# A hybrid attention step on one Trainium2 core: group A's decode is given fewer projection steps, group A's attention more; the token sums start two steps later and their tiles lie in another order

## The chip, the core and the metric

The kernel runs on one core of one Trainium2 chip. The core has five engines that work side by side, each through its own list of instructions in order: TensorE (PE; its weight loads are listed apart as PEld), VectorE (DVE), ScalarE (ACT), GpSimd (POOL) and SyncE (SP), which here issues the DMA transfers. They wait for each other by semaphores. The metric is the time of one execution on the device in microseconds (us), lower is better. Before the change it is 1755.42 us, the median of three runs (1755.3 to 1756.09).

## What is computed

One layer of a streaming encoder, on 1024 prompt tokens and on 8 requests of 16 new tokens each, which bring 1024 past tokens of cache. Everything is float32.

```python
qkv = rmsnorm(x) @ w_in                       # columns: q, k, v of group A, then of group B
# group A, 8 heads x 64: stick-breaking attention over the whole past
log_keep = where(causal, log_sigmoid(-z), 0)  # z = q k / 8
w = exp(log_sigmoid(z) + cumsum_from_the_right(log_keep) - log_keep)
# group B, 8 heads x 64: softmax over the own chunk and 8 chunks before, with a bias by distance
x = x + concat(rmsnorm(a), rmsnorm(b)) @ w_out
x = x + (silu(h @ w_gate) * (h @ w_up)) @ w_down
x = x + sigmoid(rmsnorm(x) @ w_ple_gate) * (p @ w_ple_proj)
```

Outputs are the two results and the new keys and values of both groups.

## The kernel before

Products of float32 are made from two parts: a number is split into a rounded high part (a cast on ACT) and the rest (a subtraction on DVE or POOL), and each product is three matmuls: high x high, high x low, low x high. The 1152 tokens are nine tiles of 128: eight of the prompt, one of all new tokens.

The program begins with the projection (`qkv`, line 265), a Python generator that yields after each small piece of work. Some weight chunks of 256 columns are done by a seven-product scheme (`seven`, line 420), which needs four sums of token blocks, T1 to T4, made by `sum_forms` (line 360) in steps on DVE; `beside` (line 492) takes three such steps after each step of the projection that runs meanwhile. When the scheme is done, its tiles are given back (`close_wide`, line 956), and what is left are 50 steps: 12 value steps of group A (`others`, line 308: one tile of tokens times 256 columns, 24 matmuls of 256 columns, a copy to a staging tile `st`, then a cast on ACT and a subtraction on POOL into `sv` and a store), 18 value steps of group B, and 20 steps of group B's queries (`queries`, line 282). The weights pass through one raw buffer, so a chunk's splitting (ACT and POOL) precedes the loading of the next.

Beside these 50 steps run two other generators.

- Group A's decode (`decode`, line 524): for each request four pieces of 256 cached keys and four of cached values, 512 KB each, 64 in all, through seven buffers `draw`. In each step one piece of keys is turned (L597) and scored (L619) and, six steps later, one piece of values is weighted (L606 turns the weights, L660 accumulates). 38 steps.
- The attention of the prompt (`attention`, line 707): 128 units, one per head and query tile; the first 64 are group A's. In a unit PE makes scores (L771, L772), ACT two sigmoids (`w` and `keep`, L774 and L775), DVE two running products over `keep` (L111 on the diagonal block, L114 on the rest), POOL the product of `w` and `keep` (L784); five units later PE turns the weights (L802), ACT and DVE split them, and PE multiplies with the values (L825, L826).

How they are interleaved is set by `advance(main, side, ratio, steps)` (line 924): after each step of `main`, `side` is advanced by `ratio` steps on average. In the decode stage PE's instructions stay in the order of the calls (a manual schedule); all other engines, and PE in the attention stage, are put in order by a scheduler that estimates times. Memory is given by stacks of pools: the decode's tiles lie where T1 to T4 and the scheme's other tiles were, and a tile's first write waits for the last reader of what lay there before. Attention's tiles follow where decode's were.

The calls that set the stages are these (lines 1014 to 1026):

```python
    with tc.manual_schedule(engines={mybir.EngineType.PE}):
        advance(project, dec, 1.5, 24 - 1)
        for _ in dec:
            pass
    ...
    att = run(range(8))
    advance(project, att, 2.25)
```

Of the kernel before, what the change touches and what calls it, by code (L numbers as in the profile page):

```python
# [14 lines left out]
F32R = mybir.dt.float32r  # L15
# [7 lines left out]
P = 128  # L23
D = 1024
KT = 8
# [14 lines left out]
def tile_hymba_step(  # L40
# [58 lines left out]
    def mm3(out, ah, al, bh, bl, start, stop):  # L99
        T.matmul(out, lhsT=ah, rhs=bh, start=start, stop=False)  # L100
        T.matmul(out, lhsT=ah, rhs=bl, start=False, stop=False)  # L101
        T.matmul(out, lhsT=al, rhs=bh, start=False, stop=stop)  # L102

    def sub(eng, out, a, hi):
        return eng.tensor_tensor(out, a, hi.bitcast(F32), op=ALU.subtract)  # L105
# [60 lines left out]
    def cols(w, c, n=256):  # L166
        return w[:, c * n : (c + 1) * n].rearrange("(k p) c -> p k c", p=P)
# [97 lines left out]
    def qkv(ch, hT, stg, first, second, wide):  # L265
# [35 lines left out]
        def rows_of(grp, c, st, t0, n):  # L301
            for pr in range(2):
                pt = ps["t"].tile([P, 384], F32, name="pt", tag="T")[:, : n * P]
                for o in range(n):
                    T_.transpose(pt[:, o * P : (o + 1) * P], st[:, o, pr * P : (pr + 1) * P], ident)
                transposed_out(grp, 1, c * 2 + pr, t0 * P, n * P, parts(n * P, pt))

        def others(grp, w, c, wts, gs):

            wh, wl = wts  # L310
            for g in gs:
                st = stg[0].tile([P, 3, 256], F32, name="st", tag="st", bufs=2)
                for o in range(3):
                    ps_ = ps["o"].tile([P, 256], F32, name="ps", tag="O")
                    for k in range(KT):
                        mm3(ps_, *hT.tok(g * 3 + o, k), wh[:, k], wl[:, k], k == 0, k == KT - 1)
                    (V.tensor_copy if o % 2 else A.copy)(st[:, o], ps_)  # L317
                    yield
                if w == 1:
                    rows_of(grp, c, st, g * 3, 3)  # L320
                else:
                    for o in range(3):
                        sv = stg[0].tile([P, 2, stg[1]], F32R, name="sv", tag="sq").rearrange("p a b -> p (a b)")[:, :512]
                        sv = sv.rearrange("p (h x d) -> p h x d", h=4, x=2)
                        flat = st[:, o].rearrange("p (h d) -> p h d", d=HD)
                        A.copy(sv[:, :, 0, :], flat)  # L326
                        sub(G, sv[:, :, 1, :], flat, sv[:, :, 0, :])
                        tok = slice((g * 3 + o) * P, (g * 3 + o + 1) * P)
                        nc.sync.dma_start(vhl[grp][c, tok, :], sv.bitcast(F32).rearrange("p h x d -> p (h x d)"))
                first = 4 if grp else 0  # L330
                ts_ = [t for t in range(g * 3, g * 3 + 3) if first <= t < NP]
                if ts_:
                    lo, hi = ts_[0], ts_[-1] + 1
                    nc.sync.dma_start(
                        kv_prompt[grp, w][0, 0, (lo - first) * P : (hi - first) * P, c * 4 : c * 4 + 4, :]
                        .rearrange("(t p) h d -> p t (h d)", p=P),
                        st[:, lo - g * 3 : hi - g * 3],
                    )
                if g == 2:
                    nc.sync.dma_start(  # L340
                        kv_sample[grp, w][0, :, :, c * 4 : c * 4 + 4, :].rearrange("b i h d -> (b i) (h d)"),
                        st[:, 2],
                    )

        ready, sums_of = {}, {}
# [6 lines left out]
        def load(grp, w, c, summed=False):  # L352
            if (grp, w, c) not in raws:
                fetch(grp, w, c)
            v = raws.pop((grp, w, c))
            ready[grp, w, c] = ch.parts(v, KT, 256, 4 if summed else 2)
            if summed:
                sums_of[grp, w, c] = weight_sums(wide["pool"], v)
# [130 lines left out]
        sums_ = sum_forms()  # L489
        load(0, 0, 0)  # L490

        def beside(main):
            for _ in main:
                for _ in range(3):
                    next(sums_, None)
                yield

        yield from beside(others(0, 1, 1, ready[0, 1, 1], range(3)))
        load(0, 0, 1, True)
        yield from beside(queries(0, 0, ready[0, 0, 0]))  # L500
        for _ in sums_:
            pass
# [409 lines left out]
    def pool(stack, name, side, bufs=1):  # L912
        return stack.enter_context(tc.tile_pool(name=name, bufs=bufs, side=side, reuse_waits="tile"))
# [10 lines left out]
    def advance(main, side, ratio, steps=None):  # L924

        due, n = 0.0, 0
        while steps is None or n < steps:
            if next(main, "end") == "end":
                break
            n += 1  # L930
            due += ratio
            while due >= 1.0:
                due -= 1.0
                next(side, None)
        return n
# [12 lines left out]
    wide, wstack = {}, ExitStack()  # L948

    def open_wide():  # L950
        fp = pool(wstack, "qforms", "left")
        wide["forms"] = {n: [fp.tile([P, KT // 2, 512], F32R, name=n + x) for x in "hl"] for n in ("T1", "T2", "T4", "T3")}
        wide["pool"] = pool(wstack, "qsums", "left")
        wide["banks"] = wstack.enter_context(tc.tile_pool(name="ps_w", bufs=3, space=PSUM, side="right", reuse_waits="tile"))

# [8 lines left out]
    with tc.tile_pool(name="x1", bufs=2, side="right") as xp, tc.manual_schedule(engines=all_engines):  # L964
# [28 lines left out]
        project = qkv(ch, hT, stg, w_first, ch.raw(cols(w_in[0], 3), KT, 256), wide)  # L993
# [18 lines left out]
    dp = pool(first, "dA", "left")  # L1012
    dec = decode(0, Chunks(dp, "d", 1024, RAWS, 2), dp)
    with tc.manual_schedule(engines={mybir.EngineType.PE}):
        advance(project, dec, 1.5, 24 - 1)
        for _ in dec:
            pass
    first.close()
# [4 lines left out]
    at = pool(left, "at", "left")  # L1023
    run, pairs, done = attention(at, ps, LAG)
    att = run(range(8))
    advance(project, att, 2.25)
    right.close()


# [2 lines left out]
    dec = decode(1, Chunks(dp, "d", 1024, RAWS - 1, 2), dp)  # L1032
    pp = ps["early"] = pool(dstack, "pp", "right", 2)

    def embed():

        with tc.issue_after(kept[-1].ins):
            wj = ch.load(w_ple_proj[0].rearrange("(k p) c -> p k c", p=P), 2, D)
        def turned(t):
            pn = pp.tile([P, 256], F32, name="pn", tag="pn")  # L1040
            nc.sync.dma_start(pn, p_tok[t])
            pt = ps["t"].tile([P, 512], F32, name="pt", tag="T")
            for j in range(2):
                T.transpose(pt[:, j * P : (j + 1) * P], pn[:, j * P : (j + 1) * P], ident)
            pT = [pp.tile([P, 2, P], F32R, name=f"pT{n}", tag=f"pT{n}", bufs=PT) for n in "hl"]
            pv = pt[:, :256].rearrange("p (k n) -> p k n", k=2)
            A.copy(pT[0], pv)
            sub(V, pT[1], pv, pT[0])
            return pT

        nxt = turned(0)
        yield
        for t in range(NT):
            pT = nxt
            for c in range(2):
                cs = slice(c * 512, c * 512 + 512)
                ps_ = ps["s"].tile([P, 512], F32, name="pj", tag="S")
                for k in range(2):
                    mm3(ps_, pT[0][:, k], pT[1][:, k], wj[0][:, k, cs], wj[1][:, k, cs], k == 0, k == 1)
                o = pp.tile([P, 512], F32, name="pjo", tag="pjo", bufs=2)  # L1060
                A.copy(o, ps_)
                nc.sync.dma_start(proj[t * P : (t + 1) * P, cs], o)
                if c == 0 and t + 1 < NT:
                    nxt = turned(t + 1)
                yield
# [5 lines left out]
    def along(a, b, ratio, due):  # L1071

        for _ in a:
            yield
            due += ratio
            while due >= 1.0:
                due -= 1.0
                if next(b, "end") != "end":
                    yield
        yield from b  # L1080
# [3 lines left out]
    beside = along(dec, embed(), 1.2, -3.0)  # L1084
# [84 lines left out]
    fp = pool(fstack, "forms", "left")  # L1169
# [10 lines left out]
    def form(name):  # L1180
        return [fp.tile([P, KT // 2, 512], F32R, name=name + n) for n in "hl"]
# [3 lines left out]
    T4, B22, B11, B21, T2, T3, T1 = [form(n) for n in ("T4", "B22", "B11", "B21", "T2", "T3", "T1")]  # L1185
# [300 lines left out]
    def act_place(n=D):  # L1486
        return [sA.tile([P, NT * P], F32R, name="act" + x, tag="act" + x, bufs=4)[:, :n] for x in "hl"]
# [104 lines left out]
    for d in range(nd):  # L1592
# [24 lines left out]
        S2, T2, S1, T1 = got  # L1617
# [21 lines left out]
        S3, T3, A4, T4 = got  # L1639
# [5 lines left out]
        else:  # L1645
            w_d = ch.parts(w_last, 2, D, 2, V)
            act = []
            for f in range(2):
                hl = act_place(NT * P)
# [281 lines left out]
```

## Time and profile before

| what | value |
|---|---|
| median of three runs | 1755.42 us |
| profiled execution | 1754.85 us |
| its span, first to last instruction | 1753.1 us |
| mean granted clock of TensorE | 0.98 |
| PE / PEld busy | 95% / 80% |
| DVE / ACT / POOL busy | 65% / 47% / 48% |
| first and last matmul that turns group A's cached keys (L597) | 220.6 and 353.4 us |
| last matmul on group A's cached values (L660) | 371.8 us |
| first scores of attention (L771) | 384.5 us |

The profile is one execution. Times within it count from its first instruction; the part of an execution outside the span is the difference of the second and third rows. A group of instructions is named by line, engine, operation and tiles (written <- read). An idle time is put down to what ended it. A busy share is an average over stages, so the stages are read one by one: from 220 to 376 us the decode of group A with projection steps between, from 391 to 495 us attention with the rest of the projection, from 495 to 600 us attention with little beside it, and from about 580 us on decode of group B.

### The profile page before, as it was taken

The page shows a single profiled execution, that of the slowest core. Times are in us where ns is not written, and L with a number is a line of the kernel's source. Part 1 is how long each engine was busy: PE and PEld are TensorE (multiplying, and loading weights), DVE is VectorE, ACT ScalarE, POOL GpSimd, SP SyncE. Part 2 cuts the span into 40 slices and gives each one's busy share as a digit, 9 for nine tenths or more (in the row PEclk, how much of TensorE's full clock was granted, in tenths as well). Part 3 has the DMA queues.
Part 4 walks back from the last instruction along what each step waited for, and adds up shares of the span by engine and source line. Part 5 has one row for each costly group of instructions (what it writes and reads, how often), then busy time and mean ns, then how long its engine had stood idle before and what let it go on. Part 6 is the DMA issues. An engine that isn't in the chain of part 4 may idle for free.

```text
span 1753.1 us, 27540 instructions
## 1 busy us (share of the span) xinstructions
PE 1668.3 (95%) x10064; PEld 1406.2 (80%) x10064; DVE 1144.3 (65%) x1810; ACT 831.5 (47%) x1763; POOL 849.9 (48%) x693
## 2 busy tenths in 40 slices
PE   8899899998977899889999999999999999999998
PEld 7888778887866678778778888888888878788887
DVE  6954134427889866765477666666666597798875
ACT  5433245526677767753474333333333244433663
POOL 2434222223566622312367555555555278967763
PEclk9999999999998899999999999999999999999999
DMA  5444779974583797675532222222222597722322
GB/s 188 152 143 163 255 252 326 307 202 144 139 233 100 222 278 230 176 215 173 168 133 72 94 93 93 93 94 93 94 94 93 190 385 260 269 81 77 128 96 97
DMA packets 176137, 293.48 MB, mean 167 GB/s; under 512 B 16897, under 2 KB 95489, under 8 KB 173698
## 3 DMA queue, kind: packets, MB, share of 16 engines
q1 hardware_dynamic: 176002, 291.72, 51.0%
q8 instruction: 80, 1.31, 0.3%
q14 instruction: 55, 0.45, 0.1%
HBM read 204.77 MB, written 86.90 MB: 166 GB/s over the span
## 4 chain that ended last, share of the span: by engine, by line
PE 72%; DMA 7%; DVE 5%; ACT 3%; POOL 3%; issue 2%; SPq 1%; POOLq 0%; ACTq 0%; DVEq 0%
PE ps L216 27%; PE ps L100 4%; PE ps L101 4%; PE ps L102 4%; PE pt L1536 4%; PE pt L216 3%; PE ps L1536 3%; PE pt L802 2%; DMA v<-sv 2%; PE pt L597 2%; DVE keep L114 1%; PE po L826 1%; PE po L825 1%; PE acc L660 1%; PE S L771 1%
## 5 line engine op out<-in xcount | busy, mean ns | idle before, releaser
L105 POOL TENSOR_TENSOR wlo<-wraw,whi 128x512 fp32r<-128x512 f32 (+1 forms) x127 | 219.0, 1747 | 106.3 <-ACT whi L159 103.2
L100 PE MATMUL ps<-whi,hTh 128*128 128x256 f32 x448 | 133.8, 299 | 8.1 <-ACT st L317 8.0
L102 PE MATMUL ps<-whi,hTl 128*128 128x256 f32 x448 | 130.2, 291 | 4.5 <-DVE hTl L105 4.5
L101 PE MATMUL ps<-wlo,hTh 128*128 128x256 f32 x448 | 129.8, 290 | 0.0
L159 ACT CAST whi<-wraw 128x512 fp32r<-128x512 f32 (+1 forms) x124 | 87.1, 718 | 74.7 <-PE ps L216 30.8
L784 POOL TENSOR_TENSOR w<-w,keep 128x127 f32<-128x127 f32 (+4 forms) x64 | 78.2, 1224 | 76.7 <-DVE keep L114 51.1
L802 PE MATMUL pt<-ident,w 128*128 128x128 f32 x528 | 91.3, 293 | 20.5 <-POOL w L784 8.5
L105 DVE TENSOR_TENSOR wtl<-pt,wth 128x512 fp32r<-128x512 f32 (+1 forms) x192 | 94.3, 512 | 17.9 <-ACT wth L806 17.7
L806 ACT CAST wth<-pt 128x512 fp32r<-128x512 f32 (+1 forms) x192 | 84.3, 465 | 35.8 <-PE pt L802 34.9
L100 PEld LDWEIGHTS ps<-whi,hTh 128*128 128x128 f32 x448 | 88.9, 199 | 14.8 <-ACT st L317 8.6
L114 DVE TENSOR_TENSOR_SCAN keep<-keep,zero 128x128 f32<-128x128 f32 (+7 forms) x64 | 97.9, 1531 | 1.3
L802 PEld LDWEIGHTS pt<-ident,w 128*128 128x128 f32 x528 | 65.8, 148 | 35.7 <-POOL w L784 11.4
L102 PEld LDWEIGHTS ps<-whi,hTl 128*128 128x128 f32 x448 | 88.8, 198 | 5.1 <-DVE hTl L105 5.0
L771 PE MATMUL S<-qk 128*128 128x384 f32 (+2 forms) x192 | 76.3, 400 | 14.6 <-ACT keep L775 11.5
L101 PEld LDWEIGHTS ps<-wlo,hTh 128*128 128x128 f32 x448 | 89.0, 199 | 0.4 <-issue 0.2
L825 PE MATMUL po<-wth,vk 128*128 128x256 f32 (+1 forms) x304 | 79.3, 292 | 0.4 <-DVE wtl L105 0.2
L105 POOL TENSOR_TENSOR actl<-actr,acth 128x1024 fp32r<-128x1024 f32 (+1 forms) x22 | 61.4, 2792 | 32.2 <-DMA sr<-acts 20.7
L826 PE MATMUL po<-wtl,vk 128*128 128x256 f32 (+1 forms) x304 | 74.2, 288 | 0.0
L598 DVE COPY kT<-pt 128x512 f32<-128x512 f32 x48 | 33.0, 687 | 59.7 <-PE pt L597 54.9
L105 POOL TENSOR_TENSOR S3l<-s,S3h 128x512 fp32r<-128x512 f32 x24 | 32.4, 1350 | 76.0 <-ACT S3h L236 67.9
L105 POOL TENSOR_TENSOR S2l<-s,S2h 128x512 fp32r<-128x512 f32 x24 | 35.3, 1469 | 64.8 <-PE ps L216 35.4
L105 POOL TENSOR_TENSOR sv<-st,sv 128x256 fp32r<-128x256 f32 x36 | 26.3, 734 | 79.3 <-ACT sv L326 69.5
(500 smaller groups left out, 5617.0 us busy)
## 6 DMA issues: line engine op xcount, KB each, us to landing
draw<-in_cache_sb_k SPq DMA_DIRECT2D x32, 512.0 KB, 6.7
draw<-in_cache_sb_v SPq DMA_DIRECT2D x32, 512.0 KB, 5.4
act<-sg SPq DMA_DIRECT2D x11, 1152.0 KB
actr<-act SPq DMA_DIRECT2D x22, 576.0 KB, 5.8
wraw<-in_w_in SPq DMA_DIRECT2D x11, 1024.0 KB
wraw<-in_w_gate SPq DMA_DIRECT2D x11, 1024.0 KB, 5.5
wraw<-in_w_up SPq DMA_DIRECT2D x11, 1024.0 KB
v<-sv SPq DMA_DIRECT2D x36, 256.0 KB, 5.3
```

Of the source, the lines that this page charges most:

```text
L100: T.matmul(out, lhsT=ah, rhs=bh, start=start, stop=False)
L101: T.matmul(out, lhsT=ah, rhs=bl, start=False, stop=False)
L102: T.matmul(out, lhsT=al, rhs=bh, start=False, stop=stop)
L105: return eng.tensor_tensor(out, a, hi.bitcast(F32), op=ALU.subtract)
L114: V.tensor_tensor_scan(rev, rev, zero[:, 0:1].to_broadcast([P, n - d]), keep[:, n - d : n - d + 1], op0=ALU.mult, op1=ALU.max)
L159: A.copy(h[:, o], v[:, o])
L216: T.matmul(out, lhsT=a[x][:, k], rhs=b[y][:, k], start=(not more and k == 0 and n == 0), stop=(k == 3 and n == 2), skip_group_check=more)
L771: T.matmul(sc, lhsT=hd["qq"][:, qs], rhs=hd["kkh"][:, kc], start=True, stop=False)
L802: T.transpose(pt[:, (c - c0) * P : (c - c0 + 1) * P], w[:, c * P : (c + 1) * P], ident)
L825: T.matmul(dst, lhsT=vs, rhs=wth[:, kb - base, c0:c1], start=(i == 0), stop=False)
L826: T.matmul(dst, lhsT=vs, rhs=wtl[:, kb - base, c0:c1], start=False, stop=(i == nkb - 1))
L1536: T.matmul(out, lhsT=a[i][:, x, m * P : (m + 1) * P], rhs=b[j][:, x], start=(not more and x == 0 and n == 0), stop=(x == 1 and n == 2), sk ...
```

## The change

Four edits. The first call of `beside` leaves out the token sums after its first two steps. The tiles of T1 to T4 are allocated in the order T2, T3, T1, T4, the order in which the scheme reads them. The decode of group A runs beside 11 projection steps in place of 23, at 3.2 decode steps to each in place of 1.5. The attention runs beside what is then left, 38 steps in place of 26, at 1.54 units to each in place of 2.25. No computation is added or left out.

```diff
-        def beside(main):
-            for _ in main:
-                for _ in range(3):
+        def beside(main, idle=0):
+            for n, _ in enumerate(main):
+                for _ in range(3 if n >= idle else 0):
                     next(sums_, None)
                 yield
 
-        yield from beside(others(0, 1, 1, ready[0, 1, 1], range(3)))
+        yield from beside(others(0, 1, 1, ready[0, 1, 1], range(3)), 2)
...
-        wide["forms"] = {n: [fp.tile([P, KT // 2, 512], F32R, name=n + x) for x in "hl"] for n in ("T1", "T2", "T4", "T3")}
+        wide["forms"] = {n: [fp.tile([P, KT // 2, 512], F32R, name=n + x) for x in "hl"] for n in ("T2", "T3", "T1", "T4")}
...
-        advance(project, dec, 1.5, 24 - 1)
+        advance(project, dec, 3.2, 12 - 1)
...
-    advance(project, att, 2.25)
+    advance(project, att, 1.54)
```

In the lists of instructions, everything up to the start of the decode stands as before on all engines. From there they differ. First ACT's list at the start of the decode, before and then changed (`st` is the staging of a projection step, `sv` its split values, `kT` turned keys of the cache, `qbd` the decode's queries, `wdec` its scores):

```order
L326 CAST sv_2006<-st_1919 128x4x64
L317 COPY st_2012<-ps_2065 128x256
L326 CAST sv_2091<-st_2012 128x4x64
L588 COPY qbd0_2208<-sq0_2181 64x4x16 x2
L588 COPY qbd1_2209<-sq0_2181 64x4x16 x2
L326 CAST sv_2095<-st_2012 128x4x64
L326 CAST sv_2099<-st_2012 128x4x64
L317 COPY st_2112<-ps_2113 128x256
```

```order
L317 COPY st_2012<-ps_2065 128x256
L326 CAST sv_2091<-st_2012 128x4x64
L598 COPY kT_2216<-pt_2217 128x4x128
L588 COPY qbd0_2208<-sq0_2181 64x4x16 x2
L588 COPY qbd1_2209<-sq0_2181 64x4x16 x2
L598 COPY kT_2231<-pt_2232 128x4x128
L621 ACT_TABLE_LOAD
L621 ACTIVATE wdec_2214<-sdec_2244 128x256
```

The first turned keys and scores of the decode now stand ahead of the last value casts and of the next projection step's copy, which came first before.

Next SP's list in the middle of the decode, before and then changed (`draw` is a piece of cache, `v0` the store of a value step, `mixs0` the decode's output, `out_3` the new values):

```order
L329 DMA v0_78<-sv_3084 128x512
L141 DMA draw_2931<-in_cache_sb_v 128x2x512
L141 DMA draw_2966<-in_cache_sb_k 128x2x512
L329 DMA v0_78<-sv_3088 128x512
L141 DMA draw_2968<-in_cache_sb_v 128x2x512
L141 DMA draw_3041<-in_cache_sb_k 128x2x512
L141 DMA draw_3043<-in_cache_sb_v 128x2x512
L678 DMA mixs0_111<-ow_3006 8x16x64
L334 DMA out_3<-st_2828 128x3x256
```

```order
L329 DMA v0_78<-sv_3394 128x512
L141 DMA draw_2990<-in_cache_sb_v 128x2x512
L141 DMA draw_3025<-in_cache_sb_k 128x2x512
L141 DMA draw_3027<-in_cache_sb_v 128x2x512
L141 DMA draw_3100<-in_cache_sb_k 128x2x512
L141 DMA draw_3102<-in_cache_sb_v 128x2x512
L678 DMA mixs0_111<-ow_3065 8x16x64
L141 DMA draw_3143<-in_cache_sb_k 128x2x512
L329 DMA v0_78<-sv_3398 128x512
```

Between two stores of values there are now six pieces of cache, before two to four.

Last DVE's list where the projection ends, before and then changed (L275 splits the queries' last sums, L111 opens a unit of attention, `wtl` is the low part of turned weights):

```order
L275 SCALAR_TENSOR_TENSOR sq_6641<-ps_6534,sq_6641 128x256
L841 TENSOR_REDUCE osb_5616<-pt_5624 128x4x64
L111 SCALAR_TENSOR_TENSOR keep_5541<-keep_5541,ident_60 128x128
L275 SCALAR_TENSOR_TENSOR sq_6646<-ps_6534,sq_6646 128x256
L114 SCALAR_TENSOR_TENSOR keep_5541<-keep_5541,zero_68 128x768
```

```order
L275 SCALAR_TENSOR_TENSOR sq_6641<-ps_6573,sq_6641 128x256
L105 TENSOR_TENSOR wtl_6323<-pt_6331,wth_6322 128x128
L111 SCALAR_TENSOR_TENSOR keep_6258<-keep_6258,ident_60 128x128
L105 TENSOR_TENSOR wtl_6323<-pt_6383,wth_6322 128x4x128
L105 TENSOR_TENSOR wtl_6323<-pt_6390,wth_6322 128x2x128
L111 SCALAR_TENSOR_TENSOR keep_6373<-keep_6373,ident_60 128x128
L275 SCALAR_TENSOR_TENSOR sq_6646<-ps_6573,sq_6646 128x256
```

The L111 ahead of the last L275 is the 31st of group A's 64 in the list before, and the 50th in the changed one.

## The prediction

> **What bounds the kernel now.** I read the page first (TensorE, PE, is busy 95% of the span), then cut the stretch in which the change acts into stages and asked for each engine's busy time in each. Columns: stretch, its length, busy time of each engine with its instructions, granted TensorE clock, share of the DMA engines, GB/s.
>
> ```profile
> span 1753.1 us, 27540 instructions
> PE 1668.3 (95%) x10064; PEld 1406.2 (80%) x10064; DVE 1144.3 (65%) x1810; ACT 831.5 (47%) x1763; POOL 849.9 (48%) x693
> ...
> 210.00:225.00 15.00, 8.25 (x54) 7.43 (x55) 1.81 (x3) 5.64 (x14) 6.50 (x8) 0.77 0.72 233
> 225.00:255.00 30.00, 27.23 (x263) 22.61 (x262) 9.98 (x15) 15.97 (x42) 8.70 (x8) 0.94 0.72 231
> 255.00:360.00 105.00, 104.25 (x1267) 90.71 (x1270) 49.40 (x79) 53.58 (x152) 26.85 (x37) 1.00 0.94 319
> 360.00:376.00 16.00, 16.00 (x204) 14.41 (x203) 3.26 (x10) 4.92 (x16) 4.23 (x7) 1.00 0.21 70
> 376.00:391.00 15.00, 15.00 (x95) 13.57 (x94) 1.98 (x4) 4.55 (x10) 7.48 (x8) 1.00 0.99 232
> 391.00:495.00 104.00, 97.67 (x619) 85.36 (x617) 81.46 (x125) 67.64 (x170) 45.34 (x67) 0.97 0.53 149
> 495.00:600.00 105.00, 81.72 (x515) 67.94 (x516) 97.11 (x144) 78.59 (x192) 68.12 (x86) 0.85 0.64 176
> ```
>
> From 255 to 360 us, group A's decode with projection steps between, PE is busy 104.25 of 105 us and the DMA engines run at 0.94: PE sets the pace, and the DMA queue is close behind. From 391 to 495, attention with the rest of the projection between, PE is again the fullest (97.67 of 104) with VectorE (DVE) at 81.46. From 495 to 600 the projection is used up: DVE is busy 97.11 of 105, PE 81.72 at a granted clock of 0.85. So time that PE lacks in the first two stages lies unused in the third, 105 - 81.72 = 23.3 us, and the 6.3 us of the second. Moving PE work from decode into attention is worth something only as far as it lands in that idle time.
>
> **The change part by part.** *One projection step.* In the decode stage the pieces are these (start and duration of PE instructions):
>
> ```profile
> 266.55 0.39 PE L100 MATMUL ps<-whi,hTh 128*128 128x256 f32 x1
> ...
> 269.41 0.28 PE L102 MATMUL ps<-whi,hTl 128*128 128x256 f32 x1
> 269.53 1.04 PE L597 MATMUL pt<-ident,draw 128*128 128x128 f32 x8
> 270.40 0.38 PE L606 MATMUL pt<-ident,wdec 128*128 128x128 f32 x2
> 270.72 0.67 PE L619 MATMUL sdec<-kT,qbd 128*32 128x272 f32 x8
> 271.20 0.62 PE L660 MATMUL acc<-draw,wt 128*32 128x128 f32 x16
> 271.75 0.38 PE L100 MATMUL ps<-whi,hTh 128*128 128x256 f32 x1
> ```
>
> A projection step of 24 matmuls takes 269.53 - 266.55 = 2.98 us, a decode step 271.75 - 269.53 = 2.22 us. The old ratio, 1.5 decode steps to a projection step, puts 23 projection steps beside the decode; the new, 3.2, puts 11. Twelve steps leave: 12 x 2.98 = 35.8 us of a stage that PE fills. First term: **-35.8 us**.
>
> *The DMA queue in that stage.* With fewer projection steps the cache is asked for faster. What each step moves:
>
> ```profile
> draw<-in_cache_sb_k SPq DMA_DIRECT2D x32, 512.0 KB, 6.7
> draw<-in_cache_sb_v SPq DMA_DIRECT2D x32, 512.0 KB, 5.4
> ...
> v<-sv SPq DMA_DIRECT2D x36, 256.0 KB, 5.3
> out<-st SPq DMA_DIRECT2D x8, 384.0 KB, 4.4
> ...
> L100 PE MATMUL ps<-whi,hTh 128*128 128x256 f32 x133 | 39.3, 295 | 0.0
> L619 PE MATMUL sdec<-kT,qbd 128*32 128x256 f32 (+1 forms) x192 | 15.5, 394 | 0.1
> ```
>
> The last two rows are for 255 to 360 us: 133 / 8 = 16.6 projection steps and 192 / 8 = 24 decode steps, 24 x 2.22 + 16.6 x 2.98 = 102.7 us of PE's 105. Afterwards the same 24 steps have 24 / 3.2 = 7.5 projection steps beside them: 53.3 + 22.4 = 75.7 us of PE. They still need 24 x 2 x 0.524 = 25.2 MB of cache, 7.5 x (0.262 + 0.131) = 2.9 MB of values stored twice and about 1 MB of weights: 29.1 MB, or 384 GB/s at PE's pace. The trace's rates with these transfers:
>
> ```profile
> 195.00:210.00 15.00, 13.18 (x108) 12.77 (x107) 0.42 (x1) 2.13 (x6) 3.40 (x5) 1.00 1.04 362
> 345.00:360.00 15.00, 14.25 (x171) 12.13 (x173) 8.40 (x13) 5.99 (x18) 2.20 (x4) 1.00 0.98 348
> ...
> 1402.00:1446.00 44.00, 42.81 (x188) 34.78 (x188) 40.76 (x40) 18.76 (x22) 35.47 (x14) 1.00 1.03 385
> ```
>
> At 362 GB/s the stretch lasts 80.4 us (4.7 over PE's time), at 348 83.6 (7.9), at the 319 of the whole old stretch 91.2 (15.5). The 385 belongs to other transfers, late in the kernel. I take 348, the stretch that is nearest in kind and saturated: **+8 us**, bounds 0 and 20, the upper for SyncE's queue (SP), which stands in order: a value store behind GpSimd's (POOL's) subtraction holds up the cache loads behind it, and they feed L597.
>
> The Trainium skill, "DMA: Bandwidth & Descriptors", section "Where 436 GB/s comes from", gives about 358 GB/s per core for HBM and 435 for the fabric, and calls the first the one that binds between HBM and SBUF. By 358 this term would be 5.6 us and the sum 2 us lower; by 435 it would be nothing. The 385 of the trace lies over its first figure.
>
> *The start of the decode.* The stage now begins one projection step earlier, and that is where PE waits:
>
> ```profile
> 215.65 0.58 PE L100 MATMUL ps<-whi,hTh 128*128 128x256 f32 x1 [6.46 <-ACT st L317]
> 220.63 0.60 PE L597 MATMUL pt<-ident,draw 128*128 128x128 f32 x4
> ...
> 210.53 1.00 ACT L588 COPY qbd<-sq 64x64 f32<-64x64 f32 x4 [3.06 <-POOL sq L560]
> 213.25 0.40 ACT L326 CAST sv<-st 128x256 fp32r<-128x256 f32 x1 [1.71 <-DMA v<-sv]
> ```
>
> The step at 215.65 waits 6.46 us for a staging copy, behind values whose store has not landed. In the changed order two decode steps stand ahead of it; their queries are there from 211.5 us (L588), so some of their 2 x 8 transposes and scores fill the gap. The same ScalarE (ACT) queue then mixes value casts with decode's copies, so not all of it is saved: **-3 us**, bounds -8 and +3.
>
> *Attention.* The 35.8 us come back here. The price is the pace of a unit, one query tile of one head, counted by the diagonal scan on DVE (the rows are of 391 to 495 and 495 to 600 us):
>
> ```profile
> L111 DVE TENSOR_TENSOR_SCAN keep<-keep,ident 128x128 f32<-128x128 f32 x29 | 19.5, 674 | 7.7 <-ACT keep L775 7.4
> ...
> L111 DVE TENSOR_TENSOR_SCAN keep<-keep,ident 128x128 f32<-128x128 f32 x33 | 20.4, 617 | 1.8 <-ACT keep L775 1.8
> ...
> POOL w L784 <- DVE keep L114: 27.9, 15, 3.1
> ...
> ACT sv L326 <- DMA v<-sv: 10.0, 1, 10.0
> ```
>
> With the projection between, a unit takes 104 / 29 = 3.59 us; without, 105 / 33 = 3.18. In the new order the last projection step stands after 50 of group A's 64 diagonal scans, in the old after 31. Nineteen more units at 0.41 us more make 7.8 us; since 35.8 us over 19 units is denser (1.9 us a unit) than what stood there before, I take **+10 us**. Lower bound 0: 23.3 + 6.3 us of PE are idle, and at a clock of 1.00 in place of 0.85 the same work leaves more. Upper bound: all 35.8. What moves along are two loads of weights (POOL splits them) and the work of twelve value steps of group B: cast on ACT, subtraction on POOL, store on SP. They queue among POOL's products of weights and keeps (L784), which are what the transposes wait for; in decode they ran beside a POOL busy 26.85 of 105 us, here 45 to 68 of 105.
>
> *Sums later, forms laid out otherwise.* DVE's order up to the decode is unchanged row for row, so a call two yields later moves nothing that DVE does: 0. The layout lets the first two cache loads wait for an earlier matmul. What they waited for:
>
> ```profile
> 188.62 0.45 SPq L280 DMA_DIRECT2D kT1l<-sq  x1
> 189.16 1.47 SPq L141 DMA_DIRECT2D draw<-in_cache_sb_k  x2
> ...
> SPq L141 <- PE pt L432: 0.4, 1, 0.4
> ```
>
> They follow at once on SP's store of keys; PE held them 0.4 us. That is the most it can bring, and the store of transposed keys behind them waits for ACT anyway: 0. No loss either, since nothing else is rearranged.
>
> **Sum.** -35.8 + 8 - 3 + 10 = -20.8 us. The profiled execution took 1754.85 us (span 1753.1, 1.75 around it), 0.6 under the median of 1755.42. 1754.85 - 20.8 = **1734 us**, 1.2% faster.
>
> **Rivals.** *The DMA queue keeps up.* If cache loads run at the 385 GB/s that the trace shows once, the second term is 0, the start saves 6 and attention costs 8: -33.8, 1721 us. For it: that row. Against: 319 to 362 in all stretches with 2 KB rows of cache, at shares of 0.94 to 1.04.
>
> *The decode becomes a DMA stage with stalls.* At 319 GB/s and with SP's order in the way the second term is 20 and the start saves nothing: -35.8 + 20 + 12 = -4, 1751 us, hardly to be told from no change. For it: a share of 0.94 already, and seven buffers of cache. Against: before, the loads landed in 5.4 to 6.7 us and PE never waited for them in 105 us.
>
> *Attention pays in full (the other side).* The filler goes where PE was full already, and values' work on POOL and ACT delays the chain scores, keep, scan, product, transpose: the place is 376 to 560 us, the price 35.8 us and more. With 8 for the DMA queue and -3 for the start it gives -35.8 + 8 - 3 + 36 = +5, and if each of the 18 value steps that then stand there adds 0.5 us of delay, another 9: 1760 to 1769 us, slower. It decides from 31 us of 35.8 on. For it: the wait of ACT for a store, 10.0 us, that the last value step of the old order shows as attention starts. Against: that store met the first heads' loads at a DMA share of 0.99, the stage as a whole is at 0.53.
>
> *It does not do what it says.* For the sums and the layout that is my forecast; the ratios do move the steps.
>
> **How the numbers follow.** Forecast 0.50 (1726 to 1746 by its own bounds), DMA queue keeps up 0.17, decode stalls 0.18, attention pays 0.15. A measurement of this kernel tells about 0.2%, 3.5 us, from no change. The first two are faster; of the third half is within 3.5 us and half faster; of the fourth 0.12 is slower and 0.03 the same. Faster 0.76, same 0.12, slower 0.12. For 8 times in 10 the range reaches a little past the second rival below and over the third above: **1717 to 1755 us**.
>
> **What would show it.** Right: the 6.46 us wait near 215 us is shorter; the last matmul on cached values (L660) ends near 342 us in place of 371.8; between there are short waits of PE for cache loads and 340 to 360 GB/s; matmuls of the projection go on until well over half of group A's attention; the stretch from the last L660 to the first group B unit is some 10 us longer, with a granted clock over 0.85. Wrong: waits of PE for `draw` of more than 20 us in sum; or DVE idle in attention behind ACT's value casts, which would be the slower case; or a decode that ends at 342 with the same total time.

## The result, and the profile after

The changed kernel takes 1733.83 us, the median of four runs (1731.71 to 1735.22), beside 1755.36 for the kernel before: a ratio of 0.9876, 95% interval 0.9859 to 0.9893. Its profiled execution took 1731.71 us, 23.1 less than the profiled one before; the spans differ by as much. The page's span and busy times after:

```profile
span 1729.9 us, 27555 instructions
PE 1657.0 (96%) x10064; PEld 1398.8 (81%) x10064; DVE 1152.0 (67%) x1810; ACT 829.9 (48%) x1763; POOL 847.7 (49%) x693
```

The same cut into stages as before, moved to where the stages now lie (columns as in the prediction):

```profile
208.00:225.00 17.00, 11.27 (x83) 8.82 (x81) 3.19 (x5) 7.99 (x21) 6.67 (x8) 0.80 0.85 294
225.00:255.00 30.00, 29.49 (x358) 24.04 (x362) 15.30 (x24) 19.52 (x54) 7.22 (x10) 1.00 0.90 291
255.00:322.00 67.00, 60.53 (x770) 48.24 (x769) 36.48 (x58) 35.02 (x102) 9.67 (x20) 0.95 0.95 330
322.00:345.00 23.00, 22.65 (x292) 19.75 (x292) 8.45 (x13) 8.75 (x25) 8.82 (x9) 1.00 0.61 207
...
391.00:495.00 104.00, 102.56 (x701) 92.97 (x699) 88.87 (x133) 73.34 (x182) 57.21 (x76) 1.00 0.50 141
495.00:528.00 33.00, 31.31 (x206) 27.44 (x206) 28.20 (x46) 23.04 (x61) 19.14 (x29) 1.00 0.55 147
528.00:577.00 49.00, 38.31 (x259) 31.54 (x257) 43.44 (x69) 38.44 (x94) 29.94 (x38) 0.86 0.88 262
...
285.00:315.00 30.00, 30.00 (x401) 25.08 (x400) 16.21 (x29) 17.49 (x52) 4.16 (x9) 1.00 1.00 355
```

The decode (208 to 345) is shorter, in attention PE is now nearly full up to 528 us, and the stretch in which it has too little to do shrank to 528 to 577. Where group A's decode ends, and where its attention begins and ends, is read from two tile views: first and last start of the last products of the decode (`acc`), and of the 64 diagonal scans (`keep`). The row between them is PE's wait for cached values (us, times). After:

```profile
L660 PE MATMUL acc<-draw,wt x512: 272/273/421, 235.7 to 344.5; 128*32 128x128 f32 x171
...
  DMA draw<-in_cache_sb_v: 0.2, 1
...
L111 DVE TENSOR_TENSOR_SCAN keep<-keep,ident x64: 392/425/2505, 359.3 to 576.4; 128x128 f32<-128x128 f32 x64
```

The second view for the kernel before, whose decode ended at 371.8:

```profile
L111 DVE TENSOR_TENSOR_SCAN keep<-keep,ident x64: 393/425/1858, 387.7 to 598.2; 128x128 f32<-128x128 f32 x64
```

So the decode ends 27.3 us earlier, attention begins 28.4 earlier, its 64 scans take 217.1 us in place of 210.5, and of the lead 21.8 us are left at the last of them. From there to the end both kernels need about the same, 1154.9 and 1153.5 us.

What PE waited for in the decode, before (205 to 372 us) and after (205 to 345); columns are the sum in us, times, and the longest:

```profile
PE ps L100 <- ACT st L317: 6.5, 1, 6.5
PE pt L606 <- POOL wn L648: 2.8, 2, 2.2
PE pt L597 <- ACT kT L598: 1.1, 1, 1.1
PE sdec L619 <- ACT keep L622: 0.6, 1, 0.6
```

```profile
PE pt L606 <- POOL wn L648: 5.2, 4, 3.2
PE ps L100 <- ACT st L317: 3.8, 1, 3.8
PE pt L597 <- DVE kT L598: 1.6, 3, 0.7
PE pt L597 <- ACT kT L598: 1.3, 2, 1.1
PE sdec L619 <- ACT keep L622: 0.9, 1, 0.9
```

No row names `draw`, and the view above has 0.2 us for it: PE hardly ever waited for a cache load. It waited for decode's own results, the copied weights `wn` above all. The longest of these waits in the timeline after:

```profile
256.64 2.33 DVE L114 TENSOR_TENSOR_SCAN keep<-keep,zero 128x1024 f32<-128x1024 f32 x1
259.01 1.24 DVE L636 TENSOR_TENSOR wdec<-wdec,keep 128x1039 f32<-128x1039 f32 x1
260.39 0.20 POOL L648 COPY wn<-wdec 128x16 f32<-128x16 f32 x1 [3.61 <-DVE wdec L636]
...
260.64 0.48 PE L606 MATMUL pt<-ident,wn 128*128 128x128 f32 x1 [3.21 <-POOL wn L648]
```

Scan, product and copy of one request take DVE and POOL from 256.64 to 260.59 us, and PE has come to the point where it needs them: with fewer projection steps between, its list reaches them sooner. Summed over the stage from the first L597 to the last L660, by the time from each PE instruction's start to the next (us; waits over 0.15 us apart, missing records not filled in; two experiments beside):

```
                       first L597  stage  projection      decode      waits
before                   220.6     151.2  71.1 (x562)   75.7 (x1160)   4.5
half the move (e5)       207.7     143.1  60.5 (x467)   76.2 (x1160)   6.4
the change               208.1     136.4  43.5 (x332)   80.2 (x1160)  12.8
values later (e3)        209.8     129.0  42.5 (x321)   76.8 (x1160)  10.0
```

Of the twelve steps one is gone ahead of the stage and 230 matmuls, 9.6 steps, in it. The rest, 34 matmuls, stands in the tail after the last L597, where PE's list takes more of the attention stage's filler than before.

### The profile page after: what moved, and what is told of

The parts are those of the page before. It is cut to its first block, busy times and chain, and to the rows that moved or that the text cites. A ratio compares the mean times of both kernels' runs of the same rounds, so it can differ in the third digit from the quotient of the medians.

```text
span 1729.9 us, 27555 instructions
## 1 busy us (share of the span) xinstructions
PE 1657.0 (96%) x10064; PEld 1398.8 (81%) x10064; DVE 1152.0 (67%) x1810; ACT 829.9 (48%) x1763; POOL 847.7 (49%) x693
## 4 chain that ended last, share of the span: by engine, by line
PE 74%; DVE 6%; DMA 6%; ACT 3%; POOL 3%; issue 2%; SPq 0%; POOLq 0%; ACTq 0%; DVEq 0%
PE ps L216 28%; PE pt L1536 5%; PE ps L100 4%; PE ps L101 4%; PE ps L102 4%; PE ps L1536 4%; PE pt L216 3%; PE pt L802 2%; PE pt L597 2%; PE po L826 1%; PE S L771 1%; PE po L825 1%; PE acc L660 1%; DVE keep L114 1%; PE S L772 1%
## 5 line engine op out<-in xcount | busy, mean ns | idle before, releaser
L100 PE MATMUL ps<-whi,hTh 128*128 128x256 f32 x448 | 131.6, 294 | 7.1 <-ACT st L317 7.0
L114 DVE TENSOR_TENSOR_SCAN keep<-keep,zero 128x128 f32<-128x128 f32 (+7 forms) x64 | 100.4, 1572 | 1.5
L771 PE MATMUL S<-qk 128*128 128x384 f32 (+2 forms) x192 | 72.8, 381 | 8.0 <-ACT keep L775 6.4
L105 POOL TENSOR_TENSOR S2l<-s,S2h 128x512 fp32r<-128x512 f32 x24 | 35.8, 1490 | 65.1 <-PE ps L216 35.4
L772 PE MATMUL S<-qk 128*128 128x384 f32 (+2 forms) x192 | 63.4, 334 | 0.6 <-DMA qk<-kT0l 0.6
```

The costliest lines, as they stand in the source:

```text
L114: V.tensor_tensor_scan(rev, rev, zero[:, 0:1].to_broadcast([P, n - d]), keep[:, n - d : n - d + 1], op0=ALU.mult, op1=ALU.max)
L771: T.matmul(sc, lhsT=hd["qq"][:, qs], rhs=hd["kkh"][:, kc], start=True, stop=False)
```

## The experiments

**The ratios alone, and the sums and the layout alone.** The first takes the new ratios with the old token sums and layout, the second the reverse.

```diff
-        advance(project, dec, 1.5, 24 - 1)
+        advance(project, dec, 3.2, 12 - 1)
...
-    advance(project, att, 2.25)
+    advance(project, att, 1.54)
```

> The two ratios alone, without the later sums and without the other order of T1 to T4. Theory, as predicted: sums and layout are worth nothing, the ratios all of it: 1734 us, ratio to the kernel before 0.986 to 0.990. Rival: the sums or the layout carry part of the gain: then this run is slower than the whole change by that part, 1738 us or more, ratio 0.990 or more.

> The later sums and the other layout alone, with the old ratios. Theory: 1755 us within 2 us, ratio 0.999 to 1.001. Rival that they carry part of the gain: 1751 us or less.

Ratios alone: 1731.71 us, 0.9863 [0.9850, 0.9877]; decode ends at 345.4, the scans run from 360.1 to 577.7, within 1.3 us of the whole change. Sums and layout alone: 1755.27 us, 0.9994 [0.9985, 1.0004]. As the theory had it, all of the gain is the ratios'.

**Half of the cached values.** Only the first 128 rows of each piece of group A's cached values are loaded, and they are used twice; the other half of the cached values is left out. That takes 32 x 256 KB = 8.4 MB from the queue and nothing from PE.

```diff
-            raws[i] = ch.raw(src.rearrange("(n p) h d -> p n (h d)", p=P), 2, 512)
+            src = src.rearrange("(n p) h d -> p n (h d)", p=P)
+            raws[i] = ch.raw(src, 2, 512) if kind == "k" or grp else ch.raw(src[:, 0:1], 1, 512)
...
-            blocks = [v[:, n] for n in range(2)]
+            blocks = [v[:, n if grp else 0] for n in range(2)]
```

> The whole change, but of each piece of cached values in group A only the first 128 rows are loaded, and used twice (the second 128 rows of each piece are left out, so the new tokens' result is another): 8.4 MB of 33.5 MB of cache less, all instructions of PE the same. Theory A: the DMA queue is not the bound, last L660 stays within 2 us of 344, 1732 to 1735 us. Theory B: the stage is held by the DMA queue and its 8 us go: last L660 near 337, 1726 us.

1732.21 us, 0.9863 [0.9849, 0.9876]. A stretch of its decode, PE's first wait and the decode's end (lines are one higher here):

```profile
285.00:315.00 30.00, 30.00 (x402) 24.95 (x404) 16.82 (x29) 17.64 (x53) 4.16 (x9) 1.00 0.83 281
```

```profile
PE pt L607 <- POOL wn L649: 5.2, 4, 3.2
```

```profile
L661 PE MATMUL acc<-draw,wt x512: 272/273/421, 236.2 to 343.9; 128*32 128x128 f32 x171
```

281 GB/s at a share of 0.83 in place of 355 at 1.00, the same wait to the digit, an end 0.6 us earlier. The theory that the DMA queue is not the bound came true: full as it is, it holds up nothing here.

**Values one step later.** Group A's values follow their keys by one piece more, so that `wn` has longer to be ready.

```diff
-VLAG, AHEAD = (2, 1), 2
+VLAG, AHEAD = (3, 1), 2
```

> The whole change, with the decode's values one decode step further behind its keys (7 steps in place of 6 in group A). In the changed profile PE waits in the decode for the turned weights (wn) 3.21, 0.82, 0.82 and 0.35 us, at half clock after the first, and never for a piece of cache. Theory A (the decode is held by its own chain of weights, the DMA queue keeps up): these waits go, last L660 5 to 8 us earlier, 1726 to 1729 us, ratio 0.983 to 0.985. Theory B (the predicted 8 us belong to the DMA queue): PE then waits for cache loads in their place, 1732 to 1735 us, ratio 0.987 to 0.989.

Decode's end and the scans, in two views:

```profile
L660 PE MATMUL acc<-draw,wt x512: 272/273/297, 238.7 to 338.8; 128*32 128x128 f32 x171
...
L111 DVE TENSOR_TENSOR_SCAN keep<-keep,ident x64: 389/426/2062, 353.4 to 574.2; 128x128 f32<-128x128 f32 x64
```

```profile
PE pt L597 <- DVE kT L598: 3.8, 3, 2.7
...
PE pt L606 <- POOL wn L648: 0.5, 1, 0.5
```

The wait for `wn` falls from 5.2 to 0.5 us and the decode ends 5.7 earlier, so that chain was what held it. A part returns at once: the copy of turned keys now stands behind the same long scan on DVE, and PE waits 2.7 us for it. The total does not follow: 1731.48 us, 0.9856 [0.9840, 0.9871], so theory A was right on the decode and 2.5 us short in the total. Attention takes 220.8 us in place of 217.1, and at its last scan 2.2 of 5.7 us are left.

**Half the move.** Six of the twelve steps stay in the decode.

```diff
-        advance(project, dec, 3.2, 12 - 1)
+        advance(project, dec, 2.06, 18 - 1)
...
-    advance(project, att, 1.54)
+    advance(project, att, 1.88)
```

> The whole change with half of the move: 17 projection steps beside the decode at 2.06 decode steps each (6 of the 12 steps moved), 1.88 units beside each of the rest. Theory: the first steps that are moved are the best paid, since attention's idle time is largest and the decode's own chain is not yet short of cover: 6 x 2.98 = 17.9 us less, 3 paid in attention, 1740 us, ratio 0.990 to 0.993. Rival: the gain is in proportion, half of 21.5 us, 1745 us, ratio 0.994.

1736.92 us, 0.9893 [0.9877, 0.9909]: half of the steps bring 1.07% of the 1.2 to 1.4% that the whole brings, a little more than the theory's band.

```profile
L660 PE MATMUL acc<-draw,wt x512: 272/273/297, 237.7 to 350.8; 128*32 128x128 f32 x171
...
L111 DVE TENSOR_TENSOR_SCAN keep<-keep,ident x64: 391/423/2397, 367.4 to 579.4; 128x128 f32<-128x128 f32 x64
```

The first six steps move the decode's end by 21.0 us, the second six by 6.3. The table above has the reason: from the half to the whole, projection work in the stage falls by 17.0 us, but waits grow by 6.4 and decode's own instructions by 4.0. Its attention, 212.0 us, is 1.5 over before; the second half costs 5.1.

**Half of the products.** What paces attention? Here group B's value steps do only half of their matmuls, the other half of the sum is left out: 216 matmuls less, 26.8 us at 0.124 each, casts and stores unchanged.

```diff
-                    for k in range(KT):
+                    for k in range(KT // (1 + grp * (w == 2))):
```

> The whole change, but the 18 value steps of group B make only the first half of their products (12 matmuls of 24; the other half is left out, so group B's values are others). All else stays: casts, subtractions, stores, weights. 18 x 12 matmuls x 0.124 us = 26.8 us of PE work less in the attention stage. Theory (attention has room for most of the moved work: 6.6 us paid of 35.8): 5 us less for it, group A's last diagonal scan 5 to 8 us earlier, 1727 to 1729 us. Rival (attention is paced by PE): 20 us or more less, 1712 us or less. Rival that the values' work on ACT, POOL and SP sets the pace: no change, 1733 us.

The scans, and the engines' busy times from the first to the last of them:

```profile
L111 DVE TENSOR_TENSOR_SCAN keep<-keep,ident x64: 391/424/2023, 363.0 to 577.1; 128x128 f32<-128x128 f32 x64
```

```profile
363.00:577.10 214.10, 187.36 (x1199) 162.44 (x1199) 184.38 (x269) 149.73 (x372) 122.41 (x164) 0.94 0.63 179
```

1732.74 us, 0.9862 [0.9840, 0.9884], not to be told from the change. The scans take 214.1 us, 3.0 less, but start 3.7 us later and end 0.7 us later, so the theory is missed: the decode ends at 348.6 here, 4.1 us later, with a new wait of PE of 2.6 us for a staging copy in it. Of the 216 matmuls 184, some 22.8 us, are missing between the first and the last scan. PE's busy time there fell by only 13.8 us, from the change's 201.15 (its row stands with the next experiment but one), and its granted clock from 0.97 to 0.94; its idle time grew from 16.0 to 26.7 us. What PE no longer does is not won: matmuls alone do not set this stage's pace.

**No casts of values.** Group B's value steps store the copied sums twice, without the split: no cast on ACT, no subtraction on POOL; both stored parts are then the whole value, and the split is left out.

```diff
+                        if grp:
+                            for x in range(2):
+                                nc.sync.dma_start(vhl[grp][c, tok, :].rearrange(...)[:, :, x, :], flat)
+                            continue
```

> The whole change, but the 18 value steps of group B leave out the split of their values: no cast on ACT (0.41 us each) and no subtraction on POOL (0.73 us each); the staged values are stored twice, unsplit, by two transfers (so group B's values count double). PE's work is the same. With 26.8 us of PE work left out instead, attention became only 3 us shorter. Theory (what slows a unit beside the projection is the value steps' work on ACT and POOL, ahead of sigmoids and products): a head of attention beside value steps takes 24.5 us, as without projection, in place of 27, group A's last scan 5 to 8 us earlier, 1725 to 1728 us. Rival (the units' pace does not hang on the value steps on any engine): no change, 1731 to 1734 us.

```profile
L111 DVE TENSOR_TENSOR_SCAN keep<-keep,ident x64: 391/425/2506, 359.5 to 574.5; 128x128 f32<-128x128 f32 x64
```

1729.76 us, 0.9859 [0.9843, 0.9875]; the scans take 215.0 us, 2.1 less. The change itself, run again beside it, took 1731.46 us, 0.9864 [0.9849, 0.9879]; the two can't be told apart. The theory's 5 to 8 us did not come, so the split alone does not set the pace either. One thing limits this: 18 stores of 256 KB became 36 of 128 KB, and what these cost in turn was not measured apart.

> The whole change once more, on the same chip as the two beside it: ratio 0.986 to 0.988.

**No low part of the weights.** 88 subtractions of DVE, 45.4 us by the sum of their durations, are left out of group A's attention, and the second product takes the high part again.

```diff
-                sub(V, wtl[:, ks, qs], pv, wth[:, ks, qs])
+                if grp:
+                    sub(V, wtl[:, ks, qs], pv, wth[:, ks, qs])
...
-                T.matmul(dst, lhsT=vs, rhs=wtl[:, kb - base, c0:c1], start=False, stop=(i == nkb - 1))
+                T.matmul(dst, lhsT=vs, rhs=(wtl if grp else wth)[:, kb - base, c0:c1], start=False, stop=(i == nkb - 1))
```

> The changed kernel, but the transposed weights of group A's prompt attention get no low part: VectorE's 88 subtractions at L105 (45.4 us by the group of the changed kernel's trace, 359.3 to 576.4 us) are left out, and the second matmul reads the high part again, so that TensorE's work stays what it is. In that stretch VectorE is busy 183.3 of 217.1 us and TensorE 201.2. Theory A (VectorE's chain of copies, scans and subtractions paces a unit): unit 64 follows unit 1 after 201 us or less instead of 217, where TensorE's own work is the floor, and the median falls by 14 us or more, to 1717 or below. Theory B (no single engine paces attention: each that is relieved hands the pace to another, as TensorE did with 26.8 us less of matmuls): 212 to 217 us, TensorE's and VectorE's idle time grows, median 1726 to 1732.

Engine busy times from unit 1 to unit 64, and DVE's first wait there:

```profile
359.20:578.70 219.50, 202.25 (x1392) 181.93 (x1391) 156.33 (x183) 152.84 (x381) 134.46 (x167) 0.97 0.63 180
```

```profile
DVE keep L111 <- ACT keep L775: 42.6, 33, 4.7
```

The same two of the change:

```profile
359.30:576.40 217.10, 201.15 (x1390) 179.62 (x1389) 183.31 (x271) 153.45 (x380) 127.07 (x167) 0.97 0.64 182
```

```profile
DVE keep L111 <- ACT keep L775: 18.8, 20, 2.6
```

1733.96 us, 0.9872 [0.9851, 0.9893]. DVE is busy 27.0 us less, not 45.4: its durations overlap, and the scans that stay (L111 and L114) take 128.8 us in sum in place of 119.7. Attention takes 2.4 us more: what DVE no longer does, it waits, 42.6 us for ACT's sigmoids in place of 18.8. Theory A has fallen. B's bands are missed too, by 2.5 us in attention and 2 in the total, on the slower side; its point, that the relieved engine waits, holds.

**PE in the order of the calls.** In attention, too, PE follows the calls: four projection steps ahead, then 1.74 units to each projection step, which spreads the steps evenly; once on the change, once with the values later.

```diff
-    advance(project, att, 1.54)
+    with tc.manual_schedule(engines={mybir.EngineType.PE}):
+        advance(project, att, 0, 4)
+        advance(project, att, 1.74)
```

> The whole change, with PE's instructions in the attention stage in the order of the calls (four projection steps first, then 1.74 units to each): the last projection step stands after 56 diagonal scans in place of 50. Theory (what is left to win is PE's idle time after the projection's end, 10.7 us of the 49 us from 528 to 577, and its half clock there): group A's last scan 4 to 8 us earlier, 1726 to 1730 us. Rival: in a fixed order PE waits for late units, with projection steps behind them: slower, 1738 us or more.

> The two edits together: values one decode step later, and PE in the order of the calls in attention. If the decode's 5 us were lost because attention, after it, is held by PE in the first 48 units, both gains add: 1722 us, ratio 0.981. Rival: they do not add, because group A's end is set by something that does not move with the decode's end: 1729 us or more, ratio 0.985.

```profile
L111 DVE TENSOR_TENSOR_SCAN keep<-keep,ident x64: 392/424/1741, 358.6 to 585.0; 128x128 f32<-128x128 f32 x64
```

1751.13 us, 0.9973 [0.9960, 0.9985], and 1749.56, 0.9960 [0.9945, 0.9974]. Attention takes 226.4 us, the last projection matmul starts at 561.0 in place of 521.1. Both times lie on the side of the rivals, though the second one's reason fails: of the 3.7 us by which the later values end the decode earlier here, 2.9 are left at the last scan. PE in the order of the calls gives most of the gain back, and the scheduler's own order is better here. The edit fixes the order of the units' matmuls too, so whether the even spread or the fixed order costs the time is not shown.

**Three steps back, values later.** A version from what the runs showed: fourteen projection steps beside the decode in place of eleven, values one piece later.

```diff
-VLAG, AHEAD = (2, 1), 2
+VLAG, AHEAD = (3, 1), 2
...
-        advance(project, dec, 3.2, 12 - 1)
+        advance(project, dec, 2.52, 15 - 1)
...
-    advance(project, att, 1.54)
+    advance(project, att, 1.66)
```

> A version between: 14 projection steps beside the decode at 2.52 decode steps each, 1.66 units beside each of the rest, and the decode's values one step later. If the decode loses to its own chain only what lies beyond some 2 decode steps to a projection step, and the later values cover that, the decode ends near 344 as with the whole change, with three steps fewer for attention to take: attention 212 to 215 us, 1728 to 1730 us, ratio 0.984 to 0.986. Rival (group A's end stays at 574 to 579 us, as in all versions so far with the decode's end from 339 to 351): 1732 to 1735 us, ratio 0.987.

```profile
L660 PE MATMUL acc<-draw,wt x512: 272/273/421, 240.1 to 344.0; 128*32 128x128 f32 x171
...
L111 DVE TENSOR_TENSOR_SCAN keep<-keep,ident x64: 389/425/2050, 358.6 to 569.3; 128x128 f32<-128x128 f32 x64
```

1728.31 us, 0.9851 [0.9834, 0.9867], the lowest median of all and in the theory's band. With three steps more its decode ends as early as the change's, and its attention, 210.7 us, is 6.4 shorter. Beside the change on the same chip it is 3.2 us faster, but the intervals overlap: that it beats the change is not shown.

## Why the prediction was right or wrong

The time was forecast at 1734 us and is 1733.83. The mechanism, steps out of a stage that PE fills into one that has room, holds; one of its four terms had the wrong cause. That the two figures meet so closely is in part luck: in the table, the errors of the rows (+5.2, -1.5, -0.2, -3.4 and -2.5) partly cancel. By terms, from the profiled executions (us):

```
term                                      predicted   measured
twelve steps out of the decode              -35.8      -30.6
start of the decode                          -3         -4.5
DMA queue                                    +8          0
  in its place: late weights and copies                 +7.8
attention                                   +10         +6.6
between, and after unit 64                    0         -2.5
sum                                         -20.8      -23.2
```

**Steps out of the decode.** -2.98 ahead of the stage and -27.6 in it. Of the 5.2 us that are missing, the 34 matmuls in the tail make some 4.2 (34 x 0.124). The prediction counted the steps that the calls place, not those that PE's list takes from the next stage while the last weights are made.

**Start.** The first L597 comes 12.5 us earlier, 9.5 without the step; 5.0 of these return as new waits, 3.8 us of them the old wait for the same staging copy, now at 217.8. The size was right to 1.5 us.

**DMA queue: the step that failed.** "340 to 360 GB/s" stood in the trace, "short waits of PE for cache loads" did not. The prediction capped the rate at 348 and let PE wait for the rest. The queue ran at 355 in 30 us in which PE was busy 30.00, and with 8.4 MB of cached values less the decode ended 0.6 us earlier. In the term's place stand 3.3 us of waits (12.8 - 5.0 - 4.5) and 4.5 us by which decode's own instructions were stretched, 49 of them run at half clock behind the 3.21 us wait. That they come to 7.8, where 8 were forecast for the DMA, is chance. The trace of before showed a row of this chain, 2.8 us of PE waiting for `wn`, which the prediction did not read: when steps between two dependent pieces go, what they covered shows.

By the Trainium skill, "DMA: Bandwidth & Descriptors", section "Where 436 GB/s comes from", 358 GB/s would bind here; the values-later run moved 370 over 285 to 315 us, row below, so it does not. The Trainium skill, "Perfetto Trace Analysis", section "Roofline", has the rule that fits: a single active core can go over that share, up to about 435.

**Attention.** +6.6 against +10, bounds 0 and 35.8. Time of each head in us, by the starts of every eighth scan (head 1 from its first scan to its eighth):

```
head           1     2     3     4     5     6     7     8
before       26.6  28.1  26.7  27.6  25.5  23.5  22.7  29.8
the change   24.4  27.1  29.2  27.4  27.2  26.7  25.0  30.1
half products 21.0 32.8  23.3  28.9  26.3  27.5  23.6  30.8
```

Heads 5 and 6, which had no projection beside them and now have it, take 4.9 us more; 19 units at 0.41 us, the first part of the term, gave 7.8 for all. The 2 us more for a denser filler were not there. The reason given, that PE's idle time takes up the work, is only half of it: leaving out matmuls, or casts, or DVE's subtractions shortened attention by 3.0, 2.1 and -2.4 us. Nor has a matmul of the projection one price there: between the first and the last scan the change has 254 matmuls of the projection more than before for 6.6 us, 159 more than half the move for 5.1, 184 more than half the products for 3.0, and 51 more than the version with fourteen steps for 6.4. In the three experiments that leave work out, the relieved engine waits longer: PE is idle 26.7 us in place of 16.0, ACT waits 26.7 us in place of 18.3 for scores in the run without casts, DVE 42.6 in place of 18.8 for sigmoids. PE's matmuls, DVE's subtractions and the split of the values do not, each by itself, set the pace. ACT's sigmoids and POOL's products of `w` and `keep` were not relieved, so these, the order of the lists and the chain from scores to products are left; each of these kernels also has its own order from the scheduler, so none is shown. It stays open why the values-later version loses 3.7 us in attention and the one with fourteen steps gains 6.4.

**Sums and layout.** 0 forecast, 0.9994 [0.9985, 1.0004] measured.

**Rivals.** "The DMA queue keeps up" was right that the queue holds up nothing (at 355 GB/s over 285 to 315 us, not at 385) and wrong with its 1721 us, since another chain stood behind the queue. "The decode stalls" had stalls, but in sum 12.8 us and not from DMA. "Attention pays in full" did not happen: 6.6 of 35.8. Of the signs, the shorter wait, the end near 342 (344.5), the projection well past half of attention (47 of 64 scans) and a clock over 0.85 came; the stretch from the last L660 to the last of group A's scans grew by 5.5 us, not by some 10, and the waits for cache loads did not come.

## What to carry to other kernels

When filler is taken from between the steps of a dependent chain, price the chain itself: list what the filler covered, and take each short wait that the trace already shows as the first to grow. The first half of such a move can bring most of the gain, so try half before the whole. Before a gain is expected from a fuller engine, take work away from it in an experiment: PE was busy 102.56 of 104 us in attention, and 184 matmuls less, some 22.8 us of its work, shortened it by 3.0 and the whole not measurably.

## What the runs showed of the hardware

The DMA queue of one core kept 370 GB/s over 30 us, with rows of 2 KB from the cache and some stores of values (the values-later run), more than the 348 to 362 of the stretches before:

```profile
285.00:315.00 30.00, 29.49 (x392) 24.55 (x396) 17.85 (x29) 16.96 (x50) 4.42 (x10) 1.00 1.02 370
```

A wait of PE can cost more than itself, since a stretch at half clock (0.5 granted) may follow it, but the length of the wait alone did not decide this. After the 3.21 us wait the change's clock is 0.53 for 7 us; in the values-later run, after one of 2.7 us at the same place, it stays at 1.00. The two rows, the change first:

```profile
260.00:267.00 7.00, 6.36 (x64) 4.37 (x67) 2.41 (x7) 2.54 (x8) 1.04 (x3) 0.53 1.06 380
```

```profile
260.00:267.00 7.00, 6.97 (x88) 5.90 (x89) 3.39 (x7) 3.11 (x9) 1.04 (x3) 1.00 1.06 378
```

64 matmuls ran in place of 88. But the run with values later and PE in the order of the calls has the same wait of 2.7 us, up to 258.6 us, and half clock behind it; its decode takes 131.6 us from the first L597 to the last L660, beside 129.0 with values later alone. In the version with fourteen steps half clock stands behind a wait of 1.8 us that ends at 303.3. The rows of these two:

```profile
258.00:265.00 7.00, 6.41 (x49) 4.67 (x53) 3.07 (x4) 1.98 (x5) 0.49 (x2) 0.52 1.07 381
```

```profile
304.70:308.10 3.40, 3.40 (x32) 2.62 (x28) 0.44 (x1) 1.00 (x4) 1.24 (x2) 0.50 0.79 285
```

In the change run again, the same wait of 3.21 us was followed by 0.57 from 260 to 264 us and by 1.00 from 264 to 267, half as long as the first time.

The Trainium skill, "TensorE: Matmul & The Clock Gate", Part 1, has the clock halved after an idle window of about 3.4 us. Read as a bound on a single wait, it is not borne out by these runs: 1.8 us was enough once, and 2.7 us once was and once was not. What else decides is not shown.
